# Attention probabilities turned by VectorE blocks and GpSimd transfers instead of TensorE

## The chip, the core and the metric

The kernel runs on one core of one Trainium2 chip. A core has five engines, each with a queue of its own that it works off in order: TensorE (PE in the profile, with its weight loads as PEld), VectorE (DVE), ScalarE (ACT), GpSimd (POOL) and SyncE (SP). They exchange data through SBUF (on-chip memory of 128 partitions), TensorE's results arrive in PSUM, and DMA engines move data between SBUF and device memory. SyncE, ScalarE and GpSimd issue the DMAs. The engines wait for one another by semaphores.

The metric is the time on the device of one execution, in microseconds. The kernel before was timed in three runs; one further execution was taken by the hardware profiler, and every row of the profile comes from that one.

## What is computed

Two layers of a trunk over 256 frames of width 2048, in float32. Each layer projects its input once and runs three groups of heads side by side: chunk attention (8 heads of 128), a gated linear recurrence (GLA, 4 heads) and attention into 256 memory tokens (4 heads). Each group's output is multiplied by a SiLU gate, all are mapped back by one output projection, and a layer norm follows. The part that the change touches is chunk attention:

```python
def chunk_band_attention(q, k, v, rel_table):
    ...
    scores = jnp.einsum('bnqhd,bnkhd->bhnqk', qc, k_band).astype(jnp.float32) * (Dh ** -0.5)
    ...
    scores = jnp.where(valid[None, :, None, None, :], scores + bias[None, None], NEG_INF)
    p = jax.nn.softmax(scores, axis=-1).astype(v.dtype)
    out = jnp.einsum('bhnqk,bnkhd->bnqhd', p, v_band)
```

A chunk is 64 frames and attends to itself and up to eight chunks before it, so with 256 frames every query sees all keys up to the end of its own chunk.

## The kernel before

**Projections.** All large products run in a split form: a float32 operand is rounded to a high part, what is left becomes a low part, and three products replace one. Activations are kept in SBUF as such pairs; weights stream in. `piece` (line 128) loads a piece of weights from SyncE into `raw` (4 buffers), ScalarE rounds it to `wh` (line 116) and VectorE subtracts it to get `wl` (line 117). `ws_half` (line 240) and `as_group` (line 272) then issue the products of that piece; in `ws_half`, used for the head projections, a piece is four k-tiles of weights for 256 columns, and in `as_group` two k-tiles for up to 512 columns. After each piece they call `tick`.

**Heads between the pieces.** The heads are Python generators: GLA (line 311), chunk attention `a_head` (line 503) and memory attention `m_head` (line 537). Each issues a few instructions and yields the number of ticks after which it wants to go on. `tick` (line 52) adds its share to a clock (1 for a piece of full size, less for narrow ones), keeps up to two generators active out of the waiting list, takes the first that is due, lets it issue its next step, and returns; so at most one step is issued per tick. `finish` (line 69) ticks on without matmuls until given generators are done. TensorE and SyncE work in exactly this written order (line 49). The order on VectorE, ScalarE and GpSimd is laid out when the program is built, by a planner that estimates times; the weight pieces have priority there.

**Order in a layer.** Memory keys and values, GLA's queries and keys, then two groups of values (`values(0)`, `values(1)`). The GLA generator joins the waiting list, then follow `values(2)`, the query and key projections of chunk heads 0 to 3, which join; `values(3)`, those of heads 4 to 7, which join; the memory queries and the four memory heads; then the gates (`G_BZ`, `G_AZ0`, `G_AZ1`, `G_MZ`), each with a `finish` for the heads that it gates, and the output projection.

**One chunk head** works on `s`, a tile of 128 partitions by 384: columns 0 to 127 are the first 128 queries (on partitions) against the first 128 keys, columns 128 to 383 the other 128 queries against all 256 keys. TensorE computes the scores (lines 508 and 509), VectorE scales and adds the bias (511), takes row maxima (516), ScalarE exponentiates and sums (518), VectorE takes reciprocals (519) and multiplies (521). Three ticks after the scores TensorE turns the three 128x128 squares of `s` into PSUM (526), ScalarE copies them to SBUF as `pT` (528), and two ticks later TensorE multiplies with the values (532, 533); ScalarE copies the result out (534). `scratch` tiles come from 8 buffers, `bank` is one of 4 PSUM buffers.

**GpSimd** has little to do: it clears some tiles and issues the DMAs of small parameters and of the layer norm's rows (lines 303 to 308, 647 to 663, 879 and 880).

Of the kernel before, what the change touches and what calls it, by code (L numbers as in the profile page):

```python
# [8 lines left out]
F32 = mybir.dt.float32  # L9
# [9 lines left out]
P = 128  # L19
# [17 lines left out]
def hybrid_trunk_kernel(  # L37
# [7 lines left out]
    pe, dve, act, pool, sp = nc.tensor, nc.vector, nc.scalar, nc.gpsimd, nc.sync  # L45
# [4 lines left out]
    waiting, active, done, now = [], [], set(), [0]  # L50

    def tick(share=1.0):

        now[0] += share
        while True:
            while waiting and len(active) < 2:
                active.append((waiting.pop(0), 0))
            due = [e for e in active if e[1] <= now[0]]
            if not due:
                return  # L60
            active.remove(due[0])
            g = due[0][0]
            after = next(g, None)
            if after is not None:
                active.append((g, now[0] + after))
                return
            done.add(g)

    def finish(gens):
        while not all(g in done for g in gens):  # L70
            tick()

    def enter(name, bufs=1, **kw):
        return ctx.enter_context(tc.tile_pool(name=name, bufs=bufs, **kw))
# [7 lines left out]
    sm = enter("sm", 1)  # L82
    psd = enter("psd", 2, space=bass.MemoryType.PSUM)
    psa = enter("psa", 4, space=bass.MemoryType.PSUM)

    uid = [0]

    def nm(s):
        uid[0] += 1
        return f"{s}_{uid[0]}"  # L90

    def mm(o, l, r, start, stop):
        pe.matmul(o, l, r, start=start, stop=stop, skip_group_check=True)  # L93

    def bank():
        return psa.tile([P, 512], F32, name=nm("bk"), tag="bk")

    def scratch(shape, dtype=F32):
        return sc.tile(shape, dtype, name=nm("sc"), tag="sc")

    def small(shape, tag, bufs=1):
        return sm.tile(shape, F32, name=nm(tag), tag=tag, bufs=bufs)

    ident = cst.tile([P, P], F32, name="ident")
# [135 lines left out]
    def ws_half(src, xq):  # L240

        acc = psd.tile([P, 2, 2, T], F32, name=nm("acc"), tag="acc")
        for pc in range(4):
            wh, wl = piece(src[pc], 256, 4)
            xh, _, both = xq[pc]
            for j in range(4):
                for b in range(2):
                    mm(acc[:, b].rearrange("p h t -> p (h t)"), wh[:, j, b * P:(b + 1) * P], both[:, j], pc == j == 0, False)
                for b in range(2):
                    mm(acc[:, b, 1], wl[:, j, b * P:(b + 1) * P], xh[:, j], False, pc == j == 3)  # L250
            tick()
        return acc
# [19 lines left out]
    def as_group(src, xq, n, kp=2, first=None):  # L272

        acc = psd.tile([P, 2, 512], F32, name=nm("acc"), tag="acc")
        for pc in range(16 // kp):
            if first is not None and pc % 2 == 0:
                xq.append(load_quarter(first[pc // 2]))
            w = piece(src[pc], n, kp)
            for kk in range(kp):
                for t in range(2):  # L280
                    as_products(acc[:, t, :n], t, xq, w, pc * kp + kk, kk)
            tick(n / 512)
        return acc
# [203 lines left out]
    def gla_turned(yraw, ng, y):  # L487

        for par in range(2):
# [8 lines left out]
            dve.scalar_tensor_tensor(lo, ptv, ng[:, 0:1], hi.bitcast(F32), op0=ALU.mult, op1=ALU.subtract)  # L498
            yield 1

    SCALE = P ** -0.5

    def a_head(h, load_bias, bias, q, k, asv, y):

        if h + 2 < 8:
            load_bias(h + 2)
        pb = bank()
        mm(pb[:, 0:128], q[:, 0:128], k[:, 0:128], True, True)
        mm(pb[:, 128:384], q[:, 128:256], k, True, True)
        s = scratch([P, 384])  # L510
        dve.scalar_tensor_tensor(s, pb[:, :384], SCALE, bias[h], op0=ALU.mult, op1=ALU.add)  # L511
        mx = small([P, 2], "mx", 4)
        zs = small([P, 2], "zs", 4)
        own = (slice(0, 128), slice(128, 384))
        for t in range(2):
            dve.tensor_reduce(mx[:, t:t + 1], s[:, own[t]], AX.X, ALU.max, negate=True)  # L516
        for t in range(2):
            act.activation(s[:, own[t]], s[:, own[t]], AF.Exp, bias=mx[:, t:t + 1], accum_out=zs[:, t:t + 1])  # L518
        dve.reciprocal(zs, zs)
        for t in range(2):  # L520
            dve.tensor_scalar(s[:, own[t]], s[:, own[t]], zs[:, t:t + 1], None, op0=ALU.mult)
        yield 3

        pt = bank()
        for i in range(3):
            pe.transpose(pt[:, i * P:(i + 1) * P], s[:, i * P:(i + 1) * P], ident)  # L526
        pT = scratch([P, 384])
        act.copy(pT, pt[:, :384])
        yield 2
        po = bank()  # L530
        v0 = 528 + h * P
        mm(po[:, 0:256], asv[:, 0, v0:v0 + P], pT[:, 0:256], True, False)
        mm(po[:, 128:256], asv[:, 1, v0:v0 + P], pT[:, 256:384], False, True)
        act.copy(y, po[:, :256])
        yield 2

    def m_head(h, q, mk, mv, y):
# [11 lines left out]
        dve.tensor_reduce(mx, pb.rearrange("p (t m) -> p t m", t=2), AX.X, ALU.max, negate=True)  # L549
        dve.tensor_scalar(mx, mx, SCALE, None, op0=ALU.mult)  # L550
        s = scratch([P, 2, 256])
        for t in range(2):
            act.activation(s[:, t], pb[:, t * 256:(t + 1) * 256], AF.Exp, bias=mx[:, t:t + 1], scale=SCALE, accum_out=zs[:, t:t + 1])
        dve.reciprocal(zs, zs)
# [59 lines left out]
    def wo_pieces(l, n):  # L614

        if n < 3:
            return [w512[l, G_WO + n, pc] for pc in range(8)]
        return [[w256[l, i, pc // 2][:, pc % 2 * 512:pc % 2 * 512 + 512] for i in range(2)] for pc in range(8)]
# [141 lines left out]
    for l in range(L):  # L760
# [34 lines left out]
        asv = per.tile([P, 2, 1552], F32, name=nm("asv"), tag="asv")  # L795
# [24 lines left out]
        def load_bias(h):  # L820
            bias[h] = hd.tile([P, 384], F32, name=nm("bias"), tag="bias", bufs=4)
            sp.dma_start(bias[h], relw[l, h])
# [8 lines left out]
        for half in range(2):  # L831
            values(2 + half)
            q = heads(G_AQ0 if half == 0 else G_AQ1)
            k = heads(G_AK0 if half == 0 else G_AK1)
            gens.append([a_head(half * 4 + h, load_bias, bias, q[:, h], k[:, h], asv, yraw[1 + half][:, h]) for h in range(4)])
            waiting.extend(gens[-1])
# [36 lines left out]
        for n in range(WO_N):  # L873
            if last:
                g, b = scratch([P, 512]), scratch([P, 512])
            else:
                both = per.tile([P, 2, 512], F32, name=nm("gb"), tag=f"yr{n}")
                g, b = both[:, 0], both[:, 1]
# [3 lines left out]
            src = wo_pieces(l, n)  # L882
# [122 lines left out]
```

## Time and profile before

| | us |
|---|---|
| median of 3 runs | 925.73 |
| lowest and highest | 925.34, 926.28 |
| the profiled execution | 925.59 |
| its span (first to last instruction) | 923.8 |
| TensorE busy in the span | 916.7 |
| VectorE, ScalarE, GpSimd busy | 587.9, 498.2, 21.8 |

In the timeline, a row gives start, length, engine, line, operation, the tile written and those read, shapes, and how many instructions of a kind were merged (x3). On TensorE the recorded lengths overlap, since matmuls are pipelined: the difference between starts tells what an instruction costs. In rows of groups, the number after the bar is busy time and the mean of one in ns; after the second bar stands the engine's idle time before them and which engine's instruction ended it. Line 93 is the helper that issues every matmul, so products are told apart by their tiles: `acc` is a projection, `bk` a head's PSUM buffer, `qk` the queries and keys, `asv` the values, `sc` a scratch tile. Rows of waits give the total in us, how many times, and the longest. Rows of DMA issues give KB each and the median us from issue to landing.

### The profile page before, as it was taken

The page shows a single profiled execution, that of the slowest core. Times are in us where ns is not written, and L with a number is a line of the kernel's source. Part 1 is how long each engine was busy: PE and PEld are TensorE (multiplying, and loading weights), DVE is VectorE, ACT ScalarE, POOL GpSimd, SP SyncE. Part 2 cuts the span into 40 slices and gives each one's busy share as a digit, 9 for nine tenths or more (in the row PEclk, how much of TensorE's full clock was granted, in tenths as well). Part 3 has the DMA queues.
Part 4 walks back from the last instruction along what each step waited for, and adds up shares of the span by engine and source line. Part 5 has one row for each costly group of instructions (what it writes and reads, how often), then busy time and mean ns, then how long its engine had stood idle before and what let it go on. Part 6 is the DMA issues. An engine that isn't in the chain of part 4 may idle for free.

```text
span 923.8 us, 14249 instructions
## 1 busy us (share of the span) xinstructions
PE 916.7 (99%) x5500; PEld 806.5 (87%) x5500; DVE 587.9 (64%) x812; ACT 498.2 (54%) x714; POOL 21.8 (2%) x49
## 2 busy tenths in 40 slices
PE   9999999999999999999999999999999999999997
PEld 7889998998888888888888899889888888888885
DVE  6764478665564666555587666975655555766566
ACT  6644485484454675433566445754744555754350
POOL 1000000000000000000000000000000000110000
PEclk9999999999999999999999999999999999999999
DMA  9955865546554566756675466546555544667652
GB/s 306 334 189 174 306 207 173 161 165 194 183 162 160 171 206 200 219 193 196 227 249 164 150 205 204 193 154 196 170 193 166 164 152 160 199 222 223 198 163 92
DMA packets 71253, 178.85 MB, mean 194 GB/s; under 512 B 7304, under 2 KB 31240, under 8 KB 70928
## 3 DMA queue, kind: packets, MB, share of 16 engines
q1 hardware_dynamic: 69120, 173.30, 57.1%
q0 software_dynamic: 1920, 4.36, 1.8%
q8 instruction: 43, 0.70, 0.3%
q10 hardware_dynamic: 144, 0.26, 0.1%
q14 instruction: 26, 0.21, 0.1%
HBM read 175.77 MB, written 2.10 MB: 193 GB/s over the span
## 4 chain that ended last, share of the span: by engine, by line
PE 98%; DMA 0%; DVE 0%; ACT 0%; SPq 0%; issue 0%
PE acc L93 89%; PE bk L93 8%; PE bk L526 1%; DMA raw<-w 0%; PE bk L561 0%; PE bk L590 0%; PE bk L494 0%; PE bk L393 0%; SPq L177 0%; ACT res L746 0%; ACT wh L116 0%; DVE stats L731 0%; PE bk L340 0%; DVE res L730 0%; DVE res L682 0%
## 5 line engine op out<-in xcount | busy, mean ns | idle before, releaser
L117 DVE TENSOR_TENSOR wl<-raw,wh 128x1024 fp32r<-128x1024 f32 (+3 forms) x321 | 370.0, 1154 | 255.9 <-ACT wh L116 254.9
L116 ACT CAST wh<-raw 128x1024 fp32r<-128x1024 f32 (+3 forms) x321 | 318.7, 994 | 329.9 <-PE acc L93 236.5
L93 PE MATMUL acc<-x,wh 128*128 128x512 f32 x1248 | 398.0, 400 | 0.1
L93 PE MATMUL acc<-wh,x 128*128 128x512 f32 (+2 forms) x1236 | 357.3, 370 | 0.1
L93 PEld LDWEIGHTS acc<-x,wl 128*128 128x128 f32 x1248 | 234.4, 188 | 55.3
L93 PEld LDWEIGHTS acc<-wh,x 128*128 128x128 f32 x1236 | 227.0, 188 | 27.9 <-ACT wh L116 0.6
L93 PE MATMUL acc<-x,wl 128*128 128x256 f32 x1248 | 246.0, 278 | 0.0
L93 PE MATMUL acc<-wl,x 128*128 128x512 f32 (+2 forms) x618 | 228.0, 369 | 0.0
L93 PEld LDWEIGHTS acc<-x,wh 128*128 128x128 f32 x1248 | 192.0, 189 | 1.9 <-ACT wh L116 0.4
L93 PEld LDWEIGHTS acc<-wl,x 128*128 128x128 f32 x618 | 116.0, 188 | 15.0 <-DVE wl L117 0.9
L518 ACT ACTIVATE sc<-sc,mx 128x128 f32<-128x128 f32 (+1 forms) x32 | 14.4, 450 | 20.3 <-DVE mx L516 20.3
L511 DVE SCALAR_TENSOR_TENSOR sc<-bk,bias 128x384 f32<-128x384 f32 x16 | 8.9, 554 | 12.7 <-PE bk L93 12.7
L382 ACT ACTIVATE sc<-sc 128x512 f32<-128x512 f32 x12 | 7.6, 633 | 12.5 <-DVE sc L380 12.5
L117 DVE TENSOR_TENSOR x<-sc,x 128x512 fp32r<-128x512 f32 x20 | 13.3, 684 | 0.7 <-ACT x L116 0.7
L116 ACT CAST x<-raw 128x1024 fp32r<-128x1024 f32 x5 | 5.3, 1053 | 15.3 <-DMA raw<-memT 12.7
L117 DVE TENSOR_TENSOR x<-res,x 128x512 fp32r<-128x512 f32 (+2 forms) x14 | 10.5, 765 | 4.2 <-ACT x L116 4.1
L93 PE MATMUL bk<-qk,qk 128*128 128x128 f32 (+1 forms) x64 | 13.1, 326 | 0.0
L117 DVE TENSOR_TENSOR x<-raw,x 128x1024 fp32r<-128x1024 f32 x5 | 6.1, 1225 | 10.9 <-ACT x L116 10.9
L93 PE MATMUL bk<-sc,asv 128*128 128x256 f32 (+1 forms) x64 | 13.0, 326 | 0.0
L262 DVE SCALAR_TENSOR_TENSOR sc<-acc,sc 128x512 f32<-128x512 f32 x19 | 12.9, 681 | 0.0
L116 ACT CAST x<-sc 128x512 fp32r<-128x512 f32 x20 | 11.8, 615 | 1.3 <-DVE sc L598 1.3
L623 DVE SCALAR_TENSOR_TENSOR res<-res,acc 128x512 f32<-128x512 f32 x15 | 9.7, 684 | 4.2 <-PE acc L93 4.2
(209 smaller groups left out, 567.8 us busy)
## 6 DMA issues: line engine op xcount, KB each, us to landing
raw<-w SPq DMA_DIRECT2D x214, 512.0 KB, 3.9
raw<-w SPq DMA_DIRECT2D x64, 388.0 KB, 3.3
raw<-w SPq DMA_DIRECT2D x83, 256.0 KB, 3.2
bias<-relw SPq DMA_DIRECT2D x16, 192.0 KB, 4.1
res<-xT SPq DMA_DIRECT2D x4, 512.0 KB, 5.0
res<-xn SPq DMA_DIRECT2D x1, 2048.0 KB, 8.2
raw<-memT SPq DMA_DIRECT2D x4, 512.0 KB, 4.3
res<-memT SPq DMA_DIRECT2D x6, 256.0 KB, 6.1
```

The source lines that it names most:

```text
L93: pe.matmul(o, l, r, start=start, stop=stop, skip_group_check=True)
L116: act.copy(hi, src)
L117: dve.tensor_tensor(lo, src, hi.bitcast(F32), op=ALU.subtract)
L262: dve.scalar_tensor_tensor(dst, a, scale, dst, op0=ALU.mult, op1=ALU.add)
L382: act.activation(dd, dd, AF.Abs)
L511: dve.scalar_tensor_tensor(s, pb[:, :384], SCALE, bias[h], op0=ALU.mult, op1=ALU.add)
L518: act.activation(s[:, own[t]], s[:, own[t]], AF.Exp, bias=mx[:, t:t + 1], accum_out=zs[:, t:t + 1])
L526: pe.transpose(pt[:, i * P:(i + 1) * P], s[:, i * P:(i + 1) * P], ident)
L623: dve.scalar_tensor_tensor(r, r, ALPHA, acc, op0=ALU.mult, op1=ALU.add)
```

## The change

The three transpositions on TensorE and ScalarE's copy are gone. VectorE transposes `s` in blocks of 32x32, each block within its own 32 partitions, and writes them grouped by key block. GpSimd then issues four DMAs, one for each group of 32 partitions, that write the blocks to a buffer in device memory (3 buffers) with the keys as rows, and a fifth that reads the buffer back with the keys on the 128 partitions. `pT` now holds, per key, four query blocks of 96 numbers (three squares of 32 queries each), so the two value products read their moving operand in runs of 32 numbers, with the same number of columns as before. A head's steps are two instead of three: the values come seven ticks after the scores, with no step between. Up to three generators may be active instead of two.

```diff
-            while waiting and len(active) < 2:
+            while waiting and len(active) < 3:
...
+    drm = enter("drm", 3, space=bass.MemoryType.DRAM)
...
+    def turned(dst, src, n):
+
+        blocks = scratch([P, 4, n])
+        dve.transpose(blocks.rearrange("p b (g j) -> p g b j", j=32), src.rearrange("p (g b j) -> p g b j", b=4, j=32))
+        home = drm.tile([P, 4, n], F32, name=nm("home"), tag=f"home{n}")
+        for a in range(4):
+            pool.dma_start(home[:, a].rearrange("(b i) n -> i b n", b=4), blocks[a * 32:(a + 1) * 32])
+        pool.dma_start(dst, home)
...
-        yield 3
-
-        pt = bank()
-        for i in range(3):
-            pe.transpose(pt[:, i * P:(i + 1) * P], s[:, i * P:(i + 1) * P], ident)
-        pT = scratch([P, 384])
-        act.copy(pT, pt[:, :384])
-        yield 2
+        pT = scratch([P, 4, 96])
+        turned(pT, s, 96)
+        yield 7
         po = bank()
         v0 = 528 + h * P
-        mm(po[:, 0:256], asv[:, 0, v0:v0 + P], pT[:, 0:256], True, False)
-        mm(po[:, 128:256], asv[:, 1, v0:v0 + P], pT[:, 256:384], False, True)
+        pv, pov = pT.rearrange("p a (g j) -> p g a j", j=32), po[:, :256].rearrange("p (t a j) -> p t a j", t=2, j=32)
+        mm(pov, asv[:, 0, v0:v0 + P], pv[:, 0:2], True, False)
+        mm(pov[:, 1], asv[:, 1, v0:v0 + P], pv[:, 2], False, True)
         act.copy(y, po[:, :256])
         yield 2
```

## The prediction

> **What bounds the kernel now.** I read the page first, then who waited for whom on TensorE, then the timeline around the attention heads, then GpSimd's groups and the DMA issues.
>
> ```profile
> span 923.8 us, 14249 instructions
> ...
> PE 916.7 (99%) x5500; PEld 806.5 (87%) x5500; DVE 587.9 (64%) x812; ACT 498.2 (54%) x714; POOL 21.8 (2%) x49
> ...
> q1 hardware_dynamic: 69120, 173.30, 57.1%
> ...
> L116 ACT CAST wh<-raw 128x1024 fp32r<-128x1024 f32 (+3 forms) x321 | 318.7, 994 | 329.9 <-PE acc L93 236.5
> ```
>
> ```profile
> PE bk L93 <- DVE eps L759: 1.1, 1, 1.1
> PE bk L93 <- ACT nparts L116: 0.3, 1, 0.3
> PE bk L734 <- DVE nt L696: 0.3, 1, 0.3
> ```
>
> The second fence is every wait that the trace books on TensorE: 1.7 us in 923.8. TensorE is the bound and is never short of weights: ScalarE, which prepares them first, is idle 329.9 us ahead of that work, 236.5 of it for a buffer that TensorE still holds. So a microsecond taken out of TensorE's queue comes off the end, and a microsecond that TensorE waits is added to it. That is the whole argument; the rest is what TensorE loses and for what it may have to wait.
>
> **What the change removes from TensorE.** Three transpositions per head, 16 heads.
>
> ```profile
> L526 PE MATMUL bk<-ident,sc x48: 270/272/275, 185.3 to 738.0; 128*128 128x128 f32 x48
> ```
>
> ```profile
> 206.46 0.63 PE L93 MATMUL acc<-x,wh 128*128 128x512 f32 x2
> 206.92 0.40 PE L93 MATMUL acc<-x,wl 128*128 128x256 f32 x2
> 207.15 0.49 PE L526 MATMUL bk<-ident,sc 128*128 128x128 f32 x3
> 207.40 0.72 PE L93 MATMUL acc<-x,wh 128*128 128x512 f32 x2
> 207.96 0.40 PE L93 MATMUL acc<-x,wl 128*128 128x256 f32 x2
> 208.19 0.63 PE L93 MATMUL acc<-x,wh 128*128 128x512 f32 x2
> ```
>
> The records overlap, so starts are the price. Undisturbed, one k-tile of a projection takes 207.15 - 206.46 = 0.69 us. From 207.15 to 208.19, 1.04 us, there are one such k-tile and three transpositions: these cost 0.35. 16 x 0.35 = **5.5 us** off TensorE. The largest it could be is the recorded length of all three, 16 x 0.49 = 7.8 us. In a sentence that nothing below needs: the Trainium skill, "VectorE: DVE Perf Modes", section "The three transpose paths", has a 128x128 transposition (bf16) at 390 ns on TensorE, by which 48 of them would be an estimated 18.7 us; the row has a third of that for three, and the row decides.
>
> The two value products stay. Their moving operand is now read in runs of 32 numbers instead of in one run; no row shows such a read on TensorE. Its ends: nothing, or as much again as the product costs (about 0.7 us, below), 11 us in all. I take nothing, since the count of columns is the same.
>
> **What it adds, and where it lies.** ScalarE loses 16 copies out of PSUM. VectorE gains 16 transpositions of 128x384.
>
> ```profile
> L511 DVE SCALAR_TENSOR_TENSOR sc<-bk,bias 128x384 f32<-128x384 f32 x16 | 8.9, 554 | 12.7 <-PE bk L93 12.7
> ```
>
> The nearest row is this one, the same size on the same engine: 0.55 us, 9 us in all, on an engine that is 64% busy and works ahead of TensorE. From nothing to double is nothing on the path, but it stands in each head's chain. GpSimd gains 80 DMA issues, and the DMA engines 6.3 MB to write and read beside 173.30 MB: 3.6% more bytes, in more and smaller rows (384 bytes on the way out). The weights' queue at 57.1% has room.
>
> The path is touched in one place: line 532's product now waits for a transfer. Behind it in TensorE's queue stands everything else. Is it there in time? I reckon TensorE's side first.
>
> ```profile
> 247.05 0.82 PE L93 MATMUL bk<-qk,qk 128*128 128x128 f32 x4
> ...
> 250.49 0.82 PE L93 MATMUL bk<-qk,qk 128*128 128x128 f32 x4
> ...
> 251.05 0.55 DVE L521 TENSOR_SCALAR sc<-sc,zs 128x128 f32<-128x128 f32 x2
> ...
> 256.36 0.55 DVE L521 TENSOR_SCALAR sc<-sc,zs 128x128 f32<-128x128 f32 x2
> ...
> 263.00 0.81 PE L93 MATMUL bk<-sc,asv 128*128 128x256 f32 x4
> ...
> 266.45 0.81 PE L93 MATMUL bk<-sc,asv 128*128 128x256 f32 x4
> ```
>
> These are heads 4 and 5. A tick of a head projection is four k-tiles, 4 x 0.69 = 2.76 us. The scores of the two heads are one tick apart: 3.44 = 2.76 + 0.68 for a head's score products; the value products likewise, 3.45, so 0.69. Check: from head 4's scores to its values lie five ticks, two scores and two groups of transpositions: 13.8 + 1.36 + 0.70 = 15.9; the trace has 15.95. Now seven ticks: 19.3, and with three heads under way two more heads' score or value products and its own: 19.3 + 3 x 0.68 = 21.4 us from the start of a head's scores to its values. Walking the tick rule of lines 52 to 67 through a layer, with these prices (a value projection's narrow ticks count 0.76, so seven ticks there hold more than seven pieces), gives the heads in this order: 0 and 1 about 6 us apart while the GLA generator is still active, 2 and 3 13 to 16 us later each, then 4, 5 and 6 in one burst 3.44 us apart, then 7 alone; the shortest distance is 20.8 (head 3), those of the burst are 21.4, the others 22.1 to 25.7 (head 0: 25.5). No `finish` has to run ticks without matmuls, before or after.
>
> The chain against it: softmax, turn, four writes, one read. Softmax from the scores' start: head 4 251.60 - 247.05 = 4.6, head 5 256.91 - 250.49 = 6.4. The worst of the run is head 1 of the second layer, queued behind the GLA's last steps:
>
> ```profile
> 652.78 0.82 PE L93 MATMUL bk<-qk,qk 128*128 128x128 f32 x4
> ...
> 661.46 0.55 DVE L521 TENSOR_SCALAR sc<-sc,zs 128x128 f32<-128x128 f32 x2
> ```
>
> 9.2 us. For a third in a burst I take 7.7, one more step of the same kind. The transfers, from GpSimd's group and the DMA issues (KB, median us from issue to landing):
>
> ```profile
> L303 POOL DMA_DIRECT2D gwraw<-gate_w x6 | 3.1, 524 | 106.0 <-PE bk L578 105.1 <-POOLq L995 0.8
> ```
>
> ```profile
> bias<-relw SPq DMA_DIRECT2D x16, 192.0 KB, 4.1
> ...
> gb<-ln_b POOLq DMA_DIRECT2D x4, 256.0 KB, 6.3
> ...
> out<-res SPq DMA_DIRECT2D x2, 128.0 KB, 1.9
> ...
> gbrow<-gbrow POOLq DMA_DIRECT2D x4, 8.0 KB, 1.7
> gb<-gate_b POOLq DMA_DIRECT2D x2, 1.0 KB, 4.1
> ng<-norm_g POOLq DMA_DIRECT2D x2, 0.5 KB, 4.6
> ```
>
> An issue holds GpSimd 0.52 us, so the fourth write starts 1.6 after the first. Nobody writes device memory from GpSimd in this trace, so a write's landing lies between 1.7 and 6.3 us; I take 4.4, between the two small transfers of 128 rows, which it is nearest to in rows. The read (192 KB) lies between 4.1 (the same size from SyncE) and 6.3; I take 5.2. So from the turned tile on: 1.6 + 4.4 + 5.2 = 11.2 us. With 0.55 for the turn: a lone head 4.6 + 0.55 + 11.2 = 16.4 against 20.8, a second one 6.4: 18.2 against 21.4, the third 19.5 against 21.4; the 9.2 case 21.0 against 22. **All in time, by 1 to 4 us.** The sum: the profiled execution is 925.59 (span 923.8 and 1.8 around it), 0.1 below the median 925.73; 925.6 - 5.5 = 920.1, and half a microsecond for what the new waits of 16 products cost at TensorE: **920.6**.
>
> **Rivals.**
>
> *The chain is late and TensorE waits (slower).* The read must wait until all four writes have landed, and GpSimd's queue is in order: while it waits, the next head's writes stand behind it, unless the builder's planner has put them ahead. Then each head holds GpSimd 1.6 + w + 0.5 us (w: landing of a write). In the burst, head 4's tile is turned at 5.2, and head 6's read lands at 5.2 + 3 x (1.6 + w) + 2 x 0.5 + r; its value products are due at 2 x 3.44 + 21.4 = 28.3. With w = r that is late from 4.3 us on, and each further microsecond costs 4 us per burst, 8 us in the two layers. At my 4.4 and 5.2: 5.2 + 18 + 1.0 + 5.2 = 29.4, 1.1 late, 2.2 us in all: still 922.8. At 5.0 for both the gain is gone; at the upper rows' 6.3: 16 us, 936. If instead the next writes go ahead of the read, the burst is late only when w + r passes 11.6. For it: the margins are thin, all the DMA engines are half busy, and w is unmeasured. Against it: the order is the planner's, and 1.9 and 1.7 are the only rows in which data leave SBUF. The Trainium skill, "DMA: Bandwidth & Descriptors", Specifications, says that rows under 512 bytes are read, modified and written, which speaks for a large w with these 384-byte rows; no row of this trace shows it. The Trainium skill's same page, section "Anatomy of one DMA", would give an estimated 2.1 us for 48 KB and 2.5 for 192 KB, by which nothing waits at all. Chance of slower by this: 0.28.
>
> *The gain is eaten and nothing is left (same).* The same mechanism between 3.2 and 6.8 us of waiting, or the wide read of the turned operand at half its upper end, or VectorE's and ScalarE's new order starving TensorE now and then: 923.8 to 927.4, at 925.6. Chance 0.15. That the weights run late speaks against itself: ScalarE waits 236.5 us for TensorE, and the added 0.55 us per head is small beside a tick.
>
> *A head's transfers stand behind another GpSimd instruction that waits long.* GpSimd does wait long:
>
> ```profile
> POOL gbrow L647 <- PE bk L93: 70.8, 1, 70.8
> POOL gbrow L662 <- PE bk L93: 51.8, 1, 51.8
> ```
>
> ```profile
> 174.85 0.82 PE L93 MATMUL bk<-qk,qk 128*128 128x128 f32 x4
> ...
> 188.97 0.20 POOL L647 MEMSET gbrow<- 128x128 f32 x1 [70.80 <-PE bk L93]
> ```
>
> If the transfers of the first layer's head 0 stood behind L647, they would start at 189.2 and end 11.2 later, at 200.4; its values are due at 174.85 + 25.5 = 200.3. L662 waits for the last memory head's scores, which stand behind head 7's values in TensorE's queue, so it can't stand ahead of head 7's transfers at all. This moves nothing, and lies within the forecast.
>
> *The change doesn't take the work from TensorE.* Excluded by the diff: there is no `pe.transpose` left in line 526's place.
>
> **How the numbers follow.** About 0.2% (1.85 us) is what a measurement of this kernel tells from no change, so 923.9 and below is faster. Forecast, 918 to 923.9 with 920.6: 0.57. Same: 0.15. Slower by late transfers: 0.28, between 927.5 and 937. The range starts at the upper end of the saving, 925.6 - 7.8 = 917.8, and goes to 934, which leaves about 0.1 out above and 0.05 below.
>
> **What would show it.** Right: no L526 on TensorE, TensorE's busy time and the span down by the same 5 us, no wait of TensorE for a transfer beyond a fraction of a microsecond, the writes landing at about 4.4 and the read at about 5. Wrong: rows "PE bk <- DMA" with microseconds each, above all at heads 5 and 6 of each layer; GpSimd's idle time put down to DMA between one head's writes and its read with the next head's writes behind it; the transfers' landing above 5 us; or the value products' starts further apart than 0.7 us, which would be the strided read.

## The result, and the profile after

The changed kernel takes 937.12 us (median of 4 runs, 936.65 to 937.59), the kernel before 925.97 beside it (4 runs, 925.34 to 926.28): the ratio is 1.0121, interval 1.0104 to 1.0139. It is slower by 11.2 us; forecast were 920.6, with a range that ended at 934. In the changed kernel the lines have moved: the matmul helper is L94, the weights' rounding L117, the emptying of an accumulator (`total`) L262 and L263, the addition of the bias L521, the block turn L505, the writes L508, the read L509.

First the page of the kernel after: the span, the busy shares, and of the 40 slices TensorE's and its granted clock.

```profile
span 935.8 us, 14327 instructions
...
PE 917.5 (98%) x5452; PEld 805.2 (86%) x5452; DVE 596.4 (64%) x828; ACT 487.3 (52%) x694; POOL 66.1 (7%) x129
...
PE   9999999999979999999999999999999799999997
...
PEclk9999999999989999999999999999999899999998
```

Two slices, one in each layer, stand out in both rows. TensorE's busy sum is no smaller than before, although 48 transpositions are gone. Who TensorE waited for, the three largest rows (total us, times, longest):

```profile
PE acc L94 <- DVE sc L263: 10.8, 2, 5.4
PE bk L94 <- DVE eps L765: 1.1, 1, 1.1
PE bk L94 <- ACT nparts L117: 0.3, 1, 0.3
```

No row names a transfer. The new row is a projection's accumulator (`acc`) that TensorE wanted to fill and VectorE's L263 had not yet emptied. TensorE's timeline around the first of the two:

```profile
267.86 0.81 PE L94 MATMUL bk<-sc,asv 128*128 128x256 f32 x4
274.09 1.19 PE L94 MATMUL acc<-wh,x 128*128 128x512 f32 x2 [5.42 <-DVE sc L263]
275.08 0.63 PE L94 MATMUL acc<-wl,x 128*128 128x512 f32 x1
275.51 1.05 PE L94 MATMUL acc<-wh,x 128*128 128x512 f32 x2
...
279.28 0.81 PE L94 MATMUL bk<-sc,asv 128*128 128x256 f32 x4
279.85 0.70 PE L94 MATMUL acc<-wh,x 128*128 128x512 f32 x2
```

Head 4's values come at 267.86, then 5.42 us of waiting. And the tick behind the wait is slow: its four k-tiles take 279.28 - 274.09 = 5.19 us instead of 4 x 0.69 = 2.76. The table by stretches (PEclk behind the busy times) shows why:

```profile
274.00:277.00 3.00, 2.91 (x7) 2.36 (x8) 1.84 (x3) 1.20 (x2) 1.85 (x4) 0.50 0.35 74
277.00:280.00 3.00, 3.00 (x11) 2.43 (x11) 0.00 (x0) 0.79 (x1) 0.56 (x1) 0.64 0.24 66
280.00:283.00 3.00, 3.00 (x15) 2.46 (x15) 1.23 (x1) 0.81 (x3) 0.00 (x0) 1.00 0.12 27
```

TensorE comes back at half its clock. That costs another 5.19 - 2.76 = 2.4 us, which no wait row books and which counts as busy time. The same pair stands in the second layer (wait to 734.98). Why was the accumulator full? VectorE's timeline of the kernel after, from the addition of the bias of heads 4, 5 and 6 on:

```profile
247.24 0.56 DVE L521 SCALAR_TENSOR_TENSOR sc<-bk,bias 128x384 f32<-128x384 f32 x1 [0.77 <-PE bk L94]
...
258.94 0.55 DVE L521 SCALAR_TENSOR_TENSOR sc<-bk,bias 128x384 f32<-128x384 f32 x1
...
270.08 0.55 DVE L521 SCALAR_TENSOR_TENSOR sc<-bk,bias 128x384 f32<-128x384 f32 x1
...
272.79 0.58 DVE L505 STREAM_TRANSPOSE sc<-sc 128x384 f32<-128x384 f32 x1
273.30 1.25 DVE L263 SCALAR_TENSOR_TENSOR sc<-acc,sc 128x512 f32<-128x512 f32 x2
```

TensorE had begun the three heads' scores at 246.39, 249.83 and 253.27. Head 5's bias comes 9 us and head 6's 17 us behind the start of their scores, head 4's after 0.85 us. The two late rows carry no wait: each follows a weight piece directly in VectorE's queue, so the order of the queue held them up, and no row shows anything that they lacked. An emptying is a step on ScalarE (L262) and one on VectorE (L263). The memory queries' two emptyings run together, on VectorE at 273.30 behind head 6's turn and on ScalarE behind head 6's exponentials:

```profile
271.88 1.06 ACT L262 ACTIVATE sc<-acc 128x512 f32<-128x512 f32 x2
```

Before the change head 5's bias came straight behind head 4's softmax, and the first emptying ran 14 us earlier than now:

```profile
251.52 0.55 DVE L511 SCALAR_TENSOR_TENSOR sc<-bk,bias 128x384 f32<-128x384 f32 x1
...
258.95 0.68 DVE L262 SCALAR_TENSOR_TENSOR sc<-acc,sc 128x512 f32<-128x512 f32 x1
```

GpSimd's rows of the kernel after (the name in the bracket is whoever signalled last; by the times, a read waits for its writes to land) say what head 5 and head 6 stand behind:

```profile
251.84 2.18 POOL L508 DMA_DIRECT2D home<-sc  x4 [28.95 <-DVE sc L505]
257.09 0.56 POOL L509 DMA_DIRECT2D sc<-home  x1 [3.07 <-PE acc L94]
263.38 2.18 POOL L508 DMA_DIRECT2D home<-sc  x4 [5.72 <-DVE sc L505]
268.81 0.56 POOL L509 DMA_DIRECT2D sc<-home  x1 [3.26 <-PE bk L94]
...
277.81 0.56 POOL L509 DMA_DIRECT2D sc<-home  x1 [1.97 <-DMA home<-sc]
```

Head 4's read is issued at 257.09 and head 5's softmax starts at 258.94; head 5's read at 268.81, head 6's softmax at 270.08. Each head runs behind the read of the head before it. The emptying doesn't fit this as plainly: it runs at 273.30, ahead of head 6's read at 277.81. The transfers themselves (KB, median us to landing) are quick:

```profile
home<-sc POOLq DMA_DIRECT2D x64, 48.0 KB, 2.9
...
sc<-home POOLq DMA_DIRECT2D x16, 192.0 KB, 3.4
```

**The account.** Span 923.8 to 935.8: +12.0. Two waits of 5.42 and two slow ticks of 2.4 make 15.7; the transpositions that are gone take 5.6 off (measured below); together +10.1. The other 1.9 us lie in small pieces that I did not place; 0.7 of them come ahead of the first chunk head's scores, which start at 174.85 before and at 175.55 after. By starts, the price of a wait with its slow tick is 8.0: head 5's values come 279.28 - 267.86 = 11.42 behind head 4's, where the kernel with the early touch (below) has 3.42.

### The profile page after: what moved, and what is told of

Same layout as the page of the kernel before. It is cut to its first block, busy times and chain, and to the rows that moved or that the text cites. A ratio compares the mean times of both kernels' runs of the same rounds, so it can differ in the third digit from the quotient of the medians.

```text
span 935.8 us, 14327 instructions
## 1 busy us (share of the span) xinstructions
PE 917.5 (98%) x5452; PEld 805.2 (86%) x5452; DVE 596.4 (64%) x828; ACT 487.3 (52%) x694; POOL 66.1 (7%) x129
## 4 chain that ended last, share of the span: by engine, by line
PE 97%; DMA 1%; DVE 1%; ACT 0%; issue 0%; SPq 0%; DVEq 0%
PE acc L94 89%; PE bk L94 7%; DMA sc<-home 1%; PE bk L567 0%; DMA raw<-w 0%; PE bk L596 0%; PE bk L495 0%; DVE sc L263 0%; ACT sc L528 0%; PE bk L394 0%; SPq L178 0%; DVE sc L531 0%; ACT res L752 0%; ACT wh L117 0%; DVE stats L737 0%
## 5 line engine op out<-in xcount | busy, mean ns | idle before, releaser
L117 ACT CAST wh<-raw 128x1024 fp32r<-128x1024 f32 (+3 forms) x321 | 318.9, 995 | 359.4 <-PE acc L94 283.9
L94 PE MATMUL acc<-x,wh 128*128 128x512 f32 x1248 | 396.7, 399 | 0.2 <-ACT wh L117 0.2
L94 PE MATMUL acc<-wh,x 128*128 128x512 f32 (+2 forms) x1236 | 361.2, 374 | 10.8 <-DVE sc L263 10.8
L94 PEld LDWEIGHTS acc<-x,wl 128*128 128x128 f32 x1248 | 234.4, 188 | 55.2
L94 PEld LDWEIGHTS acc<-wh,x 128*128 128x128 f32 x1236 | 229.8, 190 | 39.5 <-issue 11.2
L94 PE MATMUL acc<-x,wl 128*128 128x256 f32 x1248 | 245.9, 278 | 0.0
L94 PE MATMUL acc<-wl,x 128*128 128x512 f32 (+2 forms) x618 | 230.0, 372 | 0.0
L94 PEld LDWEIGHTS acc<-x,wh 128*128 128x128 f32 x1248 | 192.0, 189 | 1.9 <-ACT wh L117 0.4
L94 PEld LDWEIGHTS acc<-wl,x 128*128 128x128 f32 x618 | 117.5, 190 | 15.6 <-DVE wl L118 1.1
L508 POOL DMA_DIRECT2D home<-sc x64 | 35.0, 554 | 325.7 <-DVE sc L505 321.4
L521 DVE SCALAR_TENSOR_TENSOR sc<-bk,bias 128x384 f32<-128x384 f32 x16 | 8.9, 555 | 10.6 <-PE bk L94 10.6
L94 PE MATMUL bk<-qk,qk 128*128 128x128 f32 (+1 forms) x64 | 13.1, 326 | 0.0
L94 PE MATMUL bk<-sc,asv 128*128 128x256 f32 (+1 forms) x64 | 13.0, 326 | 0.0
L263 DVE SCALAR_TENSOR_TENSOR sc<-acc,sc 128x512 f32<-128x512 f32 x19 | 12.8, 679 | 0.0
L94 PEld LDWEIGHTS bk<-sc,asv 128*128 128x128 f32 x64 | 11.5, 192 | 1.3
L509 POOL DMA_DIRECT2D sc<-home x16 | 9.0, 563 | 49.6 <-DMA home<-sc 22.9
```

The costliest lines, as they stand in the source:

```text
L117: act.copy(hi, src)
L263: dve.scalar_tensor_tensor(dst, a, scale, dst, op0=ALU.mult, op1=ALU.add)
L508: pool.dma_start(home[:, a].rearrange("(b i) n -> i b n", b=4), blocks[a * 32:(a + 1) * 32])
L509: pool.dma_start(dst, home)
```

## Theories

**H, the hand-out of scratch tiles.** At build time the shared `scratch` buffers are given out in the written order, and a tile is only given out when the instruction that first writes the one before has its place. `a_head` asks for `pT` right behind the softmax, but `pT`'s first writer is now the read, which comes after the whole trip. So everything that asks for a scratch tile behind it (the next head's `s`, then the tile of the memory queries' emptying) is laid out behind that read, on whatever engine it runs. Before, `pT` was asked for three ticks later and written by ScalarE's copy at once. This rule is not in the trace; it is a guess at the planner, to be tested by edits.

**Rivals.** C, the chain: the trip is long or takes the engines' time. N, the number of buffers: there are too few scratch tiles, since a head now takes three and not two. T, three heads: the third active head by itself is too much for VectorE ahead of the emptying.

## Experiments

**A pool of its own for `pT`.** Everything else as changed.

```diff
+    ptp = enter("ptp", 2)
...
-        pT = scratch([P, 4, 96])
+        pT = ptp.tile([P, 4, 96], F32, name=nm("pT"), tag="pT")
```

> The only edit to the changed kernel: the turned tile pT comes from two buffers of its own instead of the scratch buffers. Theory H (hand-out): the planner hands scratch tiles out in the written order, and pT only when its first writer, the read from device memory, is placed; so the next head's softmax and the memory queries' totals are laid out behind that read, and TensorE waits 5.4 us per layer for its accumulator and then runs 2.4 us longer on half the clock. With pT out of that line both waits go: 937.1 - 15.7 = 921.4, and TensorE's waits fall from 12.7 us to below 3. Rival C (chain): the transfers of three heads are what is late; they stay, so 934 to 938. Rival T (three heads): three active heads crowd VectorE and ScalarE; they stay three, so 932 to 938.

Measured: 920.78 (5 runs, 920.56 to 921.23), before 925.81; ratio 0.9944, interval 0.9932 to 0.9957. TensorE's waits are those of the kernel before. So the trip, the third head and VectorE's turn are all there, and the loss is gone. But the edit also adds buffers, so the next two part the number of buffers from the order.

**An early first writer, no more buffers.** One instruction added: GpSimd clears one column of `pT` as soon as it is asked for.

```diff
         pT = scratch([P, 4, 96])
+        pool.memset(pT[:, 0, 0:1], 0.0)
         turned(pT, s, 96)
```

> The only edit to the changed kernel: GpSimd clears one column of pT right where pT is taken from the scratch buffers, 16 tiny instructions more, so that pT has a first writer at once; buffers, transfers and waits on data are as in the changed kernel. Theory H: this alone cures it, 921 to 923. Rival C: nothing changes, 937 or a little more for the added instructions. Rival N (too few scratch buffers, nine tiles for three heads and one more for the totals out of eight): the tiles are held longer than before, so 937 or worse.

Measured: 920.17 (5 runs, 920.00 to 920.66); ratio 0.9939, interval 0.9926 to 0.9951. This is below both the kernel before and the changed one. VectorE's rows of this kernel:

```profile
250.51 0.58 DVE L505 STREAM_TRANSPOSE sc<-sc 128x384 f32<-128x384 f32 x1
251.02 0.52 DVE L521 SCALAR_TENSOR_TENSOR sc<-bk,bias 128x384 f32<-128x384 f32 x1
255.71 0.58 DVE L505 STREAM_TRANSPOSE sc<-sc 128x384 f32<-128x384 f32 x1
256.21 0.52 DVE L521 SCALAR_TENSOR_TENSOR sc<-bk,bias 128x384 f32<-128x384 f32 x1
...
261.11 0.68 DVE L263 SCALAR_TENSOR_TENSOR sc<-acc,sc 128x512 f32<-128x512 f32 x1
```

Head 5's bias is straight behind head 4's turn, head 6's straight behind head 5's, and the emptying is back at 261.11. A clearing whose result nothing needs is worth 17 us, and what the trace shows moved by it is the order of the others.

**Ten scratch buffers instead of eight.**

```diff
-    sc = enter("sc", 8)
+    sc = enter("sc", 10)
```

> The only edit to the changed kernel: 10 scratch buffers instead of 8. Rival N (too few buffers): nine tiles of three heads and the totals' tile now fit, so TensorE's two waits of 5.4 us go and the time falls to about 921. Theory H: not the number but the order of the hand-out matters, so 937 and the same two waits.

Measured: 937.64 (4 runs, 937.38 to 938.81); ratio 1.0128, interval 1.0114 to 1.0142. In its waits:

```profile
PE acc L94 <- DVE sc L263: 10.8, 2, 5.4
```

The same row to the digit: it is not the number of buffers.

**The saving by itself.** The kernel before without the three transpositions and ScalarE's copy; the values are multiplied with the unturned probabilities.

```diff
-        pt = bank()
-        for i in range(3):
-            pe.transpose(pt[:, i * P:(i + 1) * P], s[:, i * P:(i + 1) * P], ident)
-        pT = scratch([P, 384])
-        act.copy(pT, pt[:, :384])
+        pT = s
```

> The kernel before without the transpositions and without ScalarE's copy: the values are multiplied with the probabilities as they stand, unturned, two active heads. It measures what 48 transpositions are worth to TensorE: by my reading of starts 5.5 us, so 920.4; if instead the recorded lengths count, 918; if the removed work was hidden, 925.9.

Measured: 921.02 (5 runs, 920.21 to 921.44), ratio 0.9947, interval 0.9933 to 0.9961; span 918.2 against 923.8. The saving is 4.8 by the medians and 5.6 by the spans.

**Three active heads, nothing else.** The kernel before with the limit of the change.

```diff
-            while waiting and len(active) < 2:
+            while waiting and len(active) < 3:
```

> The kernel before with at most three generators active instead of two and nothing else of the change. Theory H: before, the tile of the turned probabilities is asked for only three ticks after the scores, and its first writer is ScalarE's copy, so nothing is held up; the same work on TensorE in another order: 925 to 927. The rival, that a third head under way is by itself what pushes the memory queries' emptying behind a head's softmax: some 5 to 11 us more, 931 to 937.

Measured: 925.83 (10 runs, 925.32 to 926.05), before 926.09; ratio 0.9997, interval 0.9987 to 1.0007. The limit alone does nothing that can be told, though three heads do run in one burst: their scores start at 247.55, 250.99 and 254.43 and the first emptying at 260.32.

**Two active heads in the changed kernel.** The same line the other way round, all else as changed.

> The changed kernel with at most two generators active instead of three; all else as changed. Theory H (each head's softmax is laid out behind the read of the head before it, because the turned tile is handed out of the shared buffers before the next head's tile and holds up the hand-out until its first writer, the read, has its place): with two heads in a burst there is one such hand-over ahead of the memory queries' emptying instead of two. In the changed kernel head 5's addition of the bias ran at 258.9 and its turn some 3.5 us later, so the emptying can run at about 263, ahead of 268.7, when TensorE came to the full accumulator. So H expects the wait of 5.4 us twice to go while the hold-up of the second head stays in the trace: 920 to 922. A rival, that the transfers by themselves take VectorE's or GpSimd's time and so hold up the emptying, expects the wait to stay: 934 to 938.

Measured: 931.75 (4 runs, 930.61 to 932.22); ratio 1.0066, interval 1.0048 to 1.0084. Both expectations missed: the wait is neither gone nor whole. Waits, and the rows of VectorE in this kernel:

```profile
PE acc L94 <- DVE sc L263: 5.8, 2, 2.9
PE bk L94 <- DMA sc<-home: 2.1, 2, 1.1
```

```profile
260.93 0.55 DVE L521 SCALAR_TENSOR_TENSOR sc<-bk,bias 128x384 f32<-128x384 f32 x1
...
264.50 0.58 DVE L505 STREAM_TRANSPOSE sc<-sc 128x384 f32<-128x384 f32 x1
265.37 1.23 DVE L118 TENSOR_TENSOR wl<-raw,wh 128x1024 fp32r<-128x1024 f32 x1 [0.29 <-ACT wh L117]
268.14 1.22 DVE L118 TENSOR_TENSOR wl<-raw,wh 128x1024 fp32r<-128x1024 f32 x1 [1.55 <-ACT wh L117]
269.29 1.28 DVE L263 SCALAR_TENSOR_TENSOR sc<-acc,sc 128x512 f32<-128x512 f32 x2
```

One hand-over fewer, as expected, but I had let the emptying follow head 5's turn (264.50). By H's own rule it is laid out behind head 5's *read*, and two more pieces of weights lie between. So part of the miss is in my use of H. But the trace does not show that order either: the emptying ran at 269.29, ahead of that read's issue at 271.57, so behind which instruction the planner put it stays open. A second cost appears too: the head after a held-up one is late with its whole chain, and now two value products do wait for their reads (1.1 us each). Of the 10.6 us of span above the kernel of the next experiment, 7.9 are these four waits; 2.7 I did not place.

**Two active heads with the early touch.** The last two edits together.

> The kernel with the turned tile touched early, with at most two generators active instead of three. Theory H: with the early touch the order is right with two or three heads, and the values still come seven ticks after the scores: 919.5 to 921, no wait of TensorE above 1.2 us. If the third head is what gives the transfers their time, TensorE waits for reads: above 922.

Measured: 920.22 (4 runs, 920.11 to 920.45); ratio 0.9940, interval 0.9925 to 0.9956, no wait above 1.1. With the order mended, two heads or three make no difference.

**No trip through device memory.** VectorE turns straight into `pT`; the five DMAs of each head are left out, so the values are multiplied with probabilities that are turned only within their blocks.

```diff
-        turned(pT, s, 96)
+        dve.transpose(pT.rearrange("p b (g j) -> p g b j", j=32), s.rearrange("p (g b j) -> p g b j", b=4, j=32))
```

> The changed kernel with the trip through device memory left out: VectorE's transposition of 32x32 blocks writes the turned tile itself, and the four writes and the read of each head are gone, so the values are multiplied with probabilities that are turned only within their blocks. Three heads, seven ticks and the eight shared buffers stay. Theory H: the turned tile's first writer is then VectorE's transposition, right behind the softmax, so nothing is held up; no wait of TensorE above 1.2 us, 919.5 to 921, and the difference from the early-touch kernel (920.2), which does the whole trip, is what the transfers by themselves cost TensorE: within 0.7. The rival, that a third head's softmax and turn on VectorE are enough to push the memory queries' emptying back: the wait of 5.4 us twice stays, 934 to 938.

Measured: 920.69 (4 runs, 920.46 to 921.02); ratio 0.9942, interval 0.9926 to 0.9959. Its waits on TensorE, but for two of 0.2 each:

```profile
PE bk L94 <- DVE eps L765: 1.1, 1, 1.1
PE bk L94 <- ACT nparts L117: 0.3, 1, 0.3
PE bk L740 <- DVE nt L702: 0.3, 1, 0.3
```

Once `pT`'s first writer sits right behind the softmax, three heads and the turn hold up nothing. And the kernel that makes the whole trip in good order is no slower than this one that leaves it out (920.17): with the values seven ticks behind the scores, the transfers by themselves cost TensorE nothing that can be measured.

**When the transfers do decide.** The early-touch kernel with the values four ticks behind the scores.

```diff
-        yield 7
+        yield 4
```

> The kernel with the turned tile touched early, with the values four ticks after the scores instead of seven. This asks when the transfers do decide. In the early-touch kernel the read of a head was issued 13.0 to 14.4 us after its scores began (11.1 for a lone head) and landed about 3.8 later, so the chain is 15 to 18 us, and the values came 20.8 to 25.8 us after the scores. Three ticks fewer take 8.3 us away: 12.5 to 17.5. So if the chain is the deadline that the prediction took it for, TensorE waits for the reads in most heads, some 0.5 to 4.5 us each (a burst of three once, since the later heads shift along): about 10 to 14 us per layer, 938 to 950 in all, more if TensorE's clock falls behind each wait. If the chain has room that the trace does not show: 920 to 925.

Measured: 954.39 (4 runs, 951.73 to 958.93); ratio 1.0314, interval 1.0278 to 1.0350, a little above the band. The profiled execution is the longest of the four, 958.93. Its largest waits, and TensorE's rows around two of them:

```profile
PE bk L94 <- DMA sc<-home: 25.9, 7, 7.5
PE bk L94 <- ACT sc L471: 1.4, 1, 1.4
```

```profile
223.78 1.62 PE L94 MATMUL bk<-sc,asv 128*128 128x256 f32 x4 [7.51 <-DMA sc<-home]
...
229.96 0.81 PE L94 MATMUL bk<-sc,asv 128*128 128x256 f32 x4
...
275.11 1.62 PE L94 MATMUL bk<-sc,asv 128*128 128x256 f32 x4 [3.37 <-DMA sc<-home]
...
281.24 0.81 PE L94 MATMUL bk<-sc,asv 128*128 128x256 f32 x4
```

The deadline is real: these are the rows "PE bk <- DMA" that the prediction named as the sign of its main rival, and they come when three ticks are taken away. Two things were expected otherwise: 7 of the 16 heads wait and not most, and the longest wait is 7.5, not 4.5. And again the clock: one tick and one head's values take 229.96 - 223.78 = 6.18 and 281.24 - 275.11 = 6.13 us, where 3.45 is the price at full clock. The four stretches behind the waits of 7.51, 3.37, 7.39 and 3.60 lose 2.7, 2.7, 2.0 and 1.6, 9.0 in all; with 27.3 of waits that is 36.3 of the 39.0 by which its span (957.1) exceeds the early-touch kernel's (918.1).

**What follows.** The buffers' number, the third head and, at seven ticks, the transfers' time are each excluded by a run. That the loss comes with the place of `pT`'s first writer is shown: the edits that give `pT` an early first writer or take it out of the shared buffers all remove it, and the two that leave it there keep all of the wait (ten buffers) or half (two heads). The planner's rule itself, that tiles are given out in order behind first writers, is inferred from this and from the starts of the softmax behind each read. It is not shown: the emptying ran ahead of the last head's read both in the changed kernel and with two heads, and no trace holds the planner's own times.

## Why the prediction was wrong, step by step

- **The saving, 5.5 us.** Right: 5.6 by the spans, 4.8 by the medians.
- **The strided operand of the value products, taken at nothing.** Right. In the early-touch kernel the burst's value products start at 267.24, 270.66 and 274.07, 3.42 and 3.41 apart, where before they were 3.45.
- **TensorE's side of the deadline.** Right: in the same kernel the burst's scores start at 245.77, 249.21 and 252.65, so the distances are 21.5, 21.5 and 21.4; foreseen were 21.4.
- **The chain.** Too dear, on the safe side: by the medians of the kernels that make the trip, writes land in 2.9 to 3.3 us instead of 4.4, the read in 3.2 to 4.3 instead of 5.2, the turn takes 0.58 instead of 0.55, an issue 0.55 instead of 0.52. In the early-touch kernel the third read of the burst is issued at 265.76 and by the median landed at 269.6: 16.9 us after its scores, foreseen 19.5, with 4.5 to spare. The prediction also left out rows of the kernel before. It called 1.9 and 1.7 the only rows in which data leave SBUF, and took 4.1 as the lowest for a read of 192 KB:

```profile
out<-res SPq DMA_DIRECT2D x6, 256.0 KB, 2.4
...
out<-res ACTq DMA_DIRECT2D x1, 256.0 KB, 3.1
lm<-lmask SPq DMA_DIRECT2D x1, 192.0 KB, 2.5
```

With these, writes of 2.4 to 3.1 and a read between 2.5 and 4.1 were to be had, and the measured 2.9 and 3.4 lie among them.

- **GpSimd's order.** In the same kernel the next head's writes do go ahead of a read that waits, the case in which the prediction had the burst in time up to a sum of 11.6. Head 0's transfers stood ahead of the long wait of the old L647, so that rival moved nothing.
- **"The path is touched in one place."** This step failed. It looked at who waits for the transfer's *data*, and that is the value products alone. It took for granted that everything else on VectorE and ScalarE keeps its place. But the read also became the first writer of a tile from buffers that all heads and `total` share, and the memory queries' first emptying moved 14 us back, from 258.95 to 273.30: TensorE waited 5.42 us in each layer for that emptying, and for no transfer. The prediction had that place in one clause, "VectorE's and ScalarE's new order starving TensorE now and then", inside a rival with a chance of 0.15 that ended at 927.4.
- **The counter-argument, "ScalarE waits 236.5 us for TensorE".** It speaks of the weights, and they were indeed never late. It says nothing about a full accumulator: that has two buffers, and its emptying stood behind a head's softmax in both engines' queues. An engine that is idle on the whole can still hold the one instruction that TensorE needs.
- **A wait was priced at its length.** Each wait of 5.42 cost 7.8, through the clock.
- **The rival that ended slower** had the right direction and the wrong place: no transfer was late. That its 936, for transfers of 6.3 us, lies near the measured 937.1 is luck.
- **The sum, 920.6.** With the order mended and everything else of the change in place it is met, 920.17. What failed is the place of other work, not the terms of the sum.

## What to carry to other kernels

When a program is laid out by a planner, a step that fetches its result from far away must not sit in a queue for buffers that others share: ask which later requests stand behind that tile, not only who reads it. If a tile is requested long before its first write, give it a pool of its own or an early writer. And price a wait of TensorE above about 3 us with the stretch at half clock behind it, 1.6 to 2.7 us here. This is one kernel and one planner; no other was run.

## What the runs showed of the hardware

**The clock after a wait.** Waits of 2.90 us (twice, in the kernel with two active heads) left the clock at full rate, as its stretches show:

```profile
267.00:270.00 3.00, 0.22 (x2) 0.02 (x1) 1.85 (x3) 2.03 (x3) 0.55 (x2) 1.00 0.81 210
270.00:273.00 3.00, 2.88 (x13) 2.40 (x14) 1.86 (x3) 1.24 (x3) 0.56 (x1) 1.00 0.82 203
```

Waits of 3.37, 3.60, 5.42 (twice), 7.39 and 7.51 were each followed by some 3 to 5.5 us at half rate, at a cost of 1.6 to 2.7 us. Behind the wait of 3.37, which ended at 275.11:

```profile
275.00:278.00 3.00, 2.89 (x9) 2.54 (x10) 0.69 (x1) 0.52 (x2) 0.52 (x1) 0.50 0.89 296
```

The cost does not grow with the wait; behind the wait of 3.60 the first four products still ran at full rate and the slow stretch came after them. The Trainium skill, "TensorE: Matmul & The Clock Gate", Part 1, says that the clock goes to half after at least one idle window of about 3.4 us and comes back after about as long a busy one, and that the window runs freely. The trace fits this roughly: no wait of up to 2.90 slowed the clock here and each from 3.37 on did, a little under the page's figure. The late start behind 3.60 would fit a free window, but no run here shows the window itself.

**Small rows to device memory.** The Trainium skill, "DMA: Bandwidth & Descriptors", Specifications, has rows under 512 bytes read, modified and written, which the prediction took as a reason for slow writes. With these 384-byte rows 48 KB landed in 2.9 us. No run here has the same bytes in longer rows, so what the short ones cost is open; the estimates from the same page's "Anatomy of one DMA", 2.1 and 2.5 us, came nearer to the 2.9 and 3.4 than the rows that I had picked, 4.4 and 5.2.
